# Transposing pairs of bf16 as float32 words in an attention score kernel

## The chip, the cores and the metric

One core of a Trainium2 chip runs the kernel. The metric is the device time of one execution in microseconds (us), as a median over several executions. The profile covers one execution, and its span is somewhat shorter than the time, 201.3 us against about 202.8. A run counts as fast when it is within 1.5% of the fastest of its kernel, and fast runs alone are compared.

The engines: PE does matmuls and transposes, DVE (VectorE) and ACT (ScalarE) copy results out of PSUM, the memory into which PE writes, POOL (GpSimd) casts, and SP issues the transfers that 16 DMA engines carry out. The granted clock is the share of its full clock that the profile shows for PE.

## The reference

```python
batch, heads, seq, dim = 8, 8, 512, 64          # q, k: float32
scale = 1.0 / np.sqrt(q.shape[-1])
return (np.einsum('bhqd,bhkd->bhqk', q, k) * scale).astype(np.float32)
```

Inputs are 2 x 8.39 MB, and the output is 67.11 MB. There is no softmax: everything computed is also written.

## The kernel before

Two batches form a unit, and there are four units. For each, q and k are loaded (4.19 MB), cast to bf16 by POOL, transposed by PE in blocks of 128x128, and copied out of PSUM into `kT` and `qz`. Each unit then has four output buffers. Each takes eight score tiles of 128x1024, filled by two matmuls, and one store of 4.19 MB. The transposes of the next unit are interleaved with the scores of the current one.

```python
big_pool   = ctx.enter_context(tc.tile_pool(name="big", bufs=3))     # loads AND output buffers
tpsum_pool = ctx.enter_context(tc.tile_pool(name="tpsum", bufs=2, space=bass.MemoryType.PSUM))
psum_pool  = ctx.enter_context(tc.tile_pool(name="psum", bufs=3, space=bass.MemoryType.PSUM))
...
# load_and_cast: contiguous bf16
xb = bf_pool.tile([P, J, 2, D], bf16, name="xb")
for s in range(2):
    pinned(nc.gpsimd.tensor_copy(out=xb[:, :, s, :],
                                 in_=xf[:, x, s].rearrange("p (j d) -> p j d", j=J)))
...
# transpose: eight bf16 blocks to a one-bank PSUM tile, then four copies out of it
for j0 in range(0, J, 8):
    tp = tpsum_pool.tile([P, 8, P], bf16, name="tp")
    for j in range(8):
        pinned(nc.tensor.transpose(out=tp[:, j, :], identity=identity, in_=...))
    yield
    yield from rearrange(tp, ...)       # four copies, all on DVE or all on ACT
...
# scores: two matmuls to a tile, one evacuation of 128x1024
ps = psum_pool.tile([P, 2, S], f32, name="ps")
for w in range(2):
    pinned(nc.tensor.matmul(out=ps[:, w, :], lhsT=qz[:, i + w, n, :], rhs=..., ...))
evacuate(o[:, x, i:i + 2, :], ps)       # ACT or DVE, in turn
```

`pinned` keeps each engine's program order. The three `big` buffers serve the four loads first and the sixteen output buffers after that. So an early output buffer waits for a cast to empty it, and a later one for a store to land. Evacuation, the copy of a filled score tile out of PSUM into an output buffer, goes to ACT, DVE, ACT, ACT, DVE, DVE in turn.

## Time and profile before

| | before |
|---|---|
| time, median of 3 | 202.77 us (202.71 to 202.97) |
| moved by DMA | 83.89 MB, 98.1% of the span of 16 engines |
| DVE / ACT / PE busy | 126.4 / 100.7 / 99.2 us |
| store, issue to landing | 21.4 us |
| copies out of the transposes | 128 of 64x512, 687 ns on DVE, 578 ns on ACT |
| casts | 16, 1896 ns each |

### The profile page before, as it was taken

Reading aid. Unit: us, or ns where it says so; the run is one execution under the profiler, and the core shown is the slowest. Engines: PE = TensorE matmul, PEld = TensorE weight load, DVE = VectorE, ACT = ScalarE, POOL = GpSimd, SP = SyncE. Lnnn points to the kernel's source line nnn. Section 1 sums busy time; section 2 is a strip of 40 time slices with the busy share of each in tenths; the row PEclk is TensorE's granted clock in tenths of the full one; section 3 lists DMA queues with packets and bytes.
Section 4 is the critical chain, followed back from the end, with each engine's and each line's share of the span. In section 5 each row is a group of like instructions: output and inputs, shape, how many; then the busy total and the mean of one; then the engine's idle time right before and its main releaser. Section 6 shows DMA issues by size and latency. Waiting matters only on the chain.

```text
span 201.3 us, 1456 instructions
## 1 busy us (share of the span) xinstructions
PE 99.2 (49%) x503; PEld 48.3 (24%) x512; DVE 126.4 (63%) x130; ACT 100.7 (50%) x129; POOL 30.6 (15%) x22
## 2 busy tenths in 40 slices
PE   0033366753976729463729554856535666710000
PEld 0033353321522414231315221432212222200000
DVE  6726659995989929796749796569635264530000
ACT  2016667786674856583837663856515341510000
POOL 1277777556000000000000000000000000000000
PEclk9999999998599996999975998888995857555555
DMA  6999999999999999999999999999999999999993
GB/s 205 430 443 430 420 433 440 420 407 427 433 436 425 422 443 427 430 423 440 430 423 433 433 430 427 440 430 423 433 436 430 410 446 433 420 423 433 433 427 163
DMA packets 5510, 83.97 MB, mean 417 GB/s; under 512 B 384, under 2 KB 384, under 8 KB 384
## 3 DMA queue, kind: packets, MB, share of 16 engines
q1 hardware_dynamic: 5504, 83.89, 98.1%
q8 instruction: 4, 0.07, 0.1%
q14 instruction: 2, 0.02, 0.0%
HBM read 16.78 MB, written 67.11 MB: 417 GB/s over the span
## 4 chain that ended last, share of the span: by engine, by line
DMA 63%; DVE 16%; PE 3%; POOL 3%; ACT 1%; POOLq 1%; issue 1%; SPq 0%; DVEq 0%; ACTq 0%
DMA out_dram<-big 43%; DMA big<-in_q_dram 20%; DVE big L66 12%; PE ps L132 3%; DVE qz L95 3%; POOL xb L82 3%; DVE kT L95 1%; ACT big L64 1%; POOLq L186 1%; SPq L78 0%; DVEq L66 0%; SPq L137 0%; ACTq L64 0%; POOLq L82 0%
## 5 line engine op out<-in xcount | busy, mean ns | idle before, releaser
L132 PE MATMUL ps<-kT,qz 128*128 128x512 bf16 x247 | 81.1, 450 | 55.1 <-ACT big L64 39.2
L66 DVE TENSOR_SCALAR big<-ps 128x1024 f32<-128x1024 f32 x64 | 76.3, 1222 | 39.9 <-DMA out_dram<-big 29.1
L64 ACT ACTIVATE big<-ps 128x1024 f32<-128x1024 f32 x64 | 63.7, 1023 | 57.0 <-DMA out_dram<-big 30.8
L132 PEld LDWEIGHTS <-qz 128*128 128x128 bf16 x256 | 27.5, 111 | 96.0 <-issue 83.2
L82 POOL CAST xb<-big 128x2048 bf16<-128x2048 f32 x16 | 29.9, 1896 | 17.6 <-DMA big<-in_k_dram 11.9
L95 DVE COPY kT<-tp 64x512 bf16<-64x512 bf16 x32 | 22.0, 687 | 6.3 <-PE tp L107 5.7
L95 ACT COPY kT<-tp 64x512 bf16<-64x512 bf16 x32 | 18.5, 578 | 14.7 <-PE tp L107 14.4
L95 DVE COPY qz<-tp 64x512 bf16<-64x512 bf16 x32 | 22.0, 687 | 3.1 <-PE tp L116 2.7
L95 ACT COPY qz<-tp 64x512 bf16<-64x512 bf16 x32 | 18.5, 578 | 3.9 <-PE tp L116 3.6
L107 PE MATMUL tp<-identity,xb 128*128 128x128 bf16 x128 | 12.0, 254 | 16.5 <-POOL xb L82 12.5
L116 PE MATMUL tp<-identity,xb 128*128 128x128 bf16 x128 | 12.8, 265 | 6.0 <-DVE kT L95 3.5
L107 PEld LDWEIGHTS <-xb 128*128 128x128 bf16 x128 | 10.5, 116 | 20.8 <-POOL xb L82 12.8
L116 PEld LDWEIGHTS <-xb 128*128 128x128 bf16 x128 | 11.3, 122 | 10.9 <-issue 8.9
L147 DVE MEMSET qz<- 128x4096 uint32 x2 | 6.9, 3472 | 2.5 <-PEq L175 1.7
L95 ACT ACT_TABLE_LOAD x1 | 1.3, 1283 | 0.7 <-PEq L175 0.7
masks.py:199 POOL TENSOR_SCALAR_AFFINE_SELECT identity<-identity 128x128 bf16<-128x128 bf16 x1 | 0.3, 294 | 0.1
masks.py:197 POOL MEMSET identity<- 128x128 bf16 x1 | 0.2, 205 | 0.3 <-POOLq L175 0.3
L175 POOL MEMSET const-float32-0.0<- 128x1 f32 x1 | 0.1, 99 | 0.2 <-issue 0.2
L175 POOL MEMSET const-bfloat16-1.0<- 128x1 bf16 x1 | 0.1, 102 | 0.0
L175 POOL MEMSET const-uint8-127<- 128x1 uint8 x1 | 0.1, 102 | 0.0
L175 POOL MEMSET const-float32-1.0<- 128x1 f32 x1 | 0.1, 99 | 0.0
## 6 DMA issues: line engine op xcount, KB each, us to landing
out_dram<-big SPq DMA_DIRECT2D x16, 4096.0 KB, 21.4
big<-in_k_dram SPq DMA_DIRECT2D x4, 2048.0 KB, 19.2
big<-in_q_dram SPq DMA_DIRECT2D x4, 2048.0 KB, 24.2
```

The costliest lines, as they stand in the source:

```text
L64: pinned(nc.scalar.mul(out=dst, in_=src, mul=scale))
L66: pinned(nc.vector.tensor_scalar(out=dst, in0=src, scalar1=scale, scalar2=None, op0=mybir.AluOpType.mult))
L82: pinned(nc.gpsimd.tensor_copy(out=xb[:, :, s, :], in_=xf[:, x, s].rearrange("p (j d) -> p j d", j=J)))
L95: pinned(copy(out=dst(s, h), in_=src[:, h]))
L107: pinned(nc.tensor.transpose(out=tp[:, j, :], identity=identity, in_=kb[:, j0 + j].rearrange("p s d -> p (s d)")))
L116: pinned(nc.tensor.transpose(out=tp[:, i, jj, :], identity=identity, in_=qb[:, RO * jj + i0 + i].rearrange("p s d -> p (s d)")))
L132: pinned(nc.tensor.matmul(out=ps[:, w, :], lhsT=qz[:, i + w, n, :], rhs=kT[:, n].rearrange("d m s j -> d (m s j)"), start=True, stop=True))
L147: nc.vector.memset(qz, 0.0)
L175: nc = _bacc.Bacc("TRN2", target_bir_lowering=False, num_devices=1)
L186: with _tile.TileContext(nc) as tc:
```

## The change

The intent is to halve the copies. A float32 word that holds two bf16 values is transposed as a unit, so one copy of 512 words carries what two copies of 512 bf16 carried. For this the cast must place two rows side by side, element by element, which makes it write bf16 at a stride of two. A transposed tile doubles from 2 KB per partition, one PSUM bank, to two. The kernel before uses 2 x 1 + 3 x 2 = 8 banks; to stay at eight, one score tile goes. Evacuation then alternates between ACT and DVE, and the steps of the transposes are placed anew between the scores.

```diff
-    psum_pool = ctx.enter_context(tc.tile_pool(name="psum", bufs=3, space=bass.MemoryType.PSUM))
+    psum_pool = ctx.enter_context(tc.tile_pool(name="psum", bufs=2, space=bass.MemoryType.PSUM))
-        if n_evac % 6 in (0, 2, 3):
+        if n_evac % 2 == 0:
             pinned(nc.scalar.mul(out=dst, in_=src, mul=scale))
...
-            xb = bf_pool.tile([P, J, 2, D], bf16, name="xb")
+            xb = bf_pool.tile([P, JP, 2, D, 2], bf16, name="xb")
+            wide = (1, RO)[x]
             for s in range(2):
-                pinned(nc.gpsimd.tensor_copy(out=xb[:, :, s, :],
-                                             in_=xf[:, x, s].rearrange("p (j d) -> p j d", j=J)))
+                pinned(nc.gpsimd.tensor_copy(
+                    out=xb[:, :, s].rearrange("p (g i) d e -> p g e i d", i=wide),
+                    in_=xf[:, x, s].rearrange("p (g e i d) -> p g e i d", e=2, i=wide, d=D)))
...
-        for j0 in range(0, J, 8):
-            tp = tpsum_pool.tile([P, 8, P], bf16, name="tp")
+        for j0 in range(0, JP, W):                 # JP = J / 2, W = 8
+            tp = tpsum_pool.tile([P, W, P], f32, name="tp")
...                                                # the same for q; identity becomes float32
-                take(ahead, 1 + (t > 0 if v == 0 else n % 4 == 3))
+                take(ahead, 1 if v == 0 else int(n in (0, 2, 3, 5, 6)))
```

## The prediction

> **What bounds the kernel now.** I read the busy table first, then the slices, the DMA queues, the chain that ended last and the waits of the queue's own engine.
>
> ```profile
> PE 99.2 (49%) x503; PEld 48.3 (24%) x512; DVE 126.4 (63%) x130; ACT 100.7 (50%) x129; POOL 30.6 (15%) x22
> ...
> DMA  6999999999999999999999999999999999999993
> GB/s 205 430 443 430 420 433 440 420 407 427 433 436 425 422 443 427 430 423 440 430 423 433 433 430 427 440 430 423 433 436 430 410 446 433 420 423 433 433 427 163
> ...
> q1 hardware_dynamic: 5504, 83.89, 98.1%
> ...
> DMA 63%; DVE 16%; PE 3%; POOL 3%; ACT 1%; POOLq 1%; issue 1%; SPq 0%; DVEq 0%; ACTq 0%
> ```
>
> No compute engine is above 63% of the span, while the 16 DMA engines are at 9 tenths or more in every slice but the first and the last, and their packets fill 98.1% of the span: at most 1.9% of 201.3 us, 3.8 us, is not transfer, and that is the first latency and the tail. The work is 83.89 MB, fixed by the inputs and the float32 output. So the bound is the DMA.
>
> How far is compute ahead of it? The page's issue part and the chain in order of time answer that:
>
> ```profile
> out_dram<-big SPq DMA_DIRECT2D x16, 4096.0 KB, 21.4
> ```
>
> ```profile
> 60.06 3.50 DVE big L66 x3
> 63.56 0.02 SPq L137
> 63.58 0.03 issue
> 63.61 20.21 DMA out_dram<-big
> 83.82 0.03 issue
> 83.85 0.05 DVEq L66
> 83.90 0.05 issue
> 83.95 1.23 DVE big L66
> ```
>
> A store of 4 MB takes 4.19 MB / 0.43 GB per ms, some 9.7 us, yet lands 21.4 us after its issue: when a store is issued, about one more is queued ahead of it, and evacuation then waits for a buffer that a store must free (in the waits, DVE stands 29.1 us and ACT 30.8 us for a store to land). The reserve per store is some 21.4 - 9.7 = 11.7 us. In the timeline the first stores are issued at 38.2, 46.1, 58.3 and 63.6 us. Counting back in steps of 9.7 us from the landing at 83.8 us of the fourth, stores land at 54.6, 64.4 and 74.1 us; so the second store had 54.6 - 46.1 = 8.5 us in hand, the third 64.4 - 58.3 = 6.1 us, the fourth 10.5 us. The first had least: all four loads, without it, end near 43 us, so some 4.8 us. The last store is issued at 178.2 us, when about 12 us of older traffic is left.
>
> **What the Trainium skill says.** "DMA: Bandwidth & Descriptors", section "Where 436 GB/s comes from", gives 435 GB/s as the ceiling of the DMA ports of a core; the slices of this trace show 407 to 446, so the queue runs at it and no rearrangement of engines adds to it. "VectorE: DVE Perf Modes", section "Why PSUM operands drop a tier", says that a float32 operand in PSUM keeps VectorE at one element per cycle. The trace has the bf16 copies at 687 ns for 512 elements, about one per cycle too, so a copy of 512 words should cost the same and carry twice the data. "TensorE: Matmul & The Clock Gate", section "Weight-path perf modes — Fast Weight Load (FWL) and DoubleRow", says that the fast weight load is off for FP32 weights; the kernel before loads only bf16 weights, so its trace can't show the float32 price. "SBUF — State Buffer", section "Door 1: The DMA port swizzle", has a note that lines are 16 bytes and that at least two hits per line keep full rate, so that eight bf16 elements is a free stride. The cast will write bf16 at a stride of two elements. No strided cast is in this trace.
>
> **The change, part by part.**
>
> ```profile
> L66 DVE TENSOR_SCALAR big<-ps 128x1024 f32<-128x1024 f32 x64 | 76.3, 1222 | 39.9 <-DMA out_dram<-big 29.1
> L64 ACT ACTIVATE big<-ps 128x1024 f32<-128x1024 f32 x64 | 63.7, 1023 | 57.0 <-DMA out_dram<-big 30.8
> ...
> L82 POOL CAST xb<-big 128x2048 bf16<-128x2048 f32 x16 | 29.9, 1896 | 17.6 <-DMA big<-in_k_dram 11.9
> L95 DVE COPY kT<-tp 64x512 bf16<-64x512 bf16 x32 | 22.0, 687 | 6.3 <-PE tp L107 5.7
> L95 ACT COPY kT<-tp 64x512 bf16<-64x512 bf16 x32 | 18.5, 578 | 14.7 <-PE tp L107 14.4
> ```
>
> *Copies.* 128 copies of 64x512 bf16 become 64 copies of 64x512 words at the same estimated 687 and 578 ns. DVE loses 32 x 0.687 = 22 us, ACT 32 x 0.578 = 18.5 us. That is all off the path, except in the prologue, where copies lie in series with the transposes (13.6 to 29.4 us): four bursts of copies in place of eight, so scores start some 4 to 6 us earlier. The first output buffer is freed only by the cast of the second load, at 27.1 us, so the first store gains about 2 us at most, into a queue that is full anyway.
>
> *Transposes.* 256 of bf16 become 128 of float32. Eight took 0.61 us in the timeline, 76 ns apart. Without the fast load, and with weights that may not be loaded ahead, I guess 200 to 300 ns each, a burst of eight 1.6 to 2.4 us, in PE's program order ahead of the next scores.
>
> *Score tiles.* With three, the fourth store's tile, which had no copies beside it, was filled in 63.6 - 58.3 = 5.3 us: four DVE evacuations of 1.23 us back to back. With two, and evacuation strictly alternating, each engine owns one tile: evacuation 1.23 us, then two matmuls 0.61 us, then about 0.1 us of signals, 1.95 us a round, so 4 x 1.95 = 7.8 us for an output buffer. The remaining copies (0.69 us) fit into the refill gap of 0.7 us. One burst per output buffer adds 1.6 to 2.4 us less the half microsecond or so that PE has idle in a round: 9 to 10 us while the next unit is prepared, 7.8 us in the last unit (up to 9 at the low clock).
>
> *Against the queue.* A store takes 9.7 us. Filling at 9 to 10 us runs about level with it, and a burst of 10.5 us for eight buffers would eat 8 x 0.8 = 6.4 us of a reserve of 10 to 12. The last unit earns it back. So the sum on the path that sets the end is zero.
>
> *Casts.* Sixteen as before. At 1.9 us each nothing moves. POOL has 4.9 us per load of 2 MB for two casts of 3.75 us, so up to about 2.4 us each would still be hidden.
>
> **The rivals.**
> 1. *The strided casts are slow.* At 3.8 us each POOL would need 16 x 3.8 = 61 us from 8.7 us, so the last ends at 69.5, not 48.8. The first store waits for the eighth cast, at 39.1 us, and is issued near 48; the loads end at 43; the second and third stores also come late, some 5 us each. The end: about 216 us. Against it: [...]the note on 16-byte lines. I give it some 6%.
> 2. *Compute becomes the bound.* A float32 transpose at 500 ns makes a burst of 4 us and a fill of 11.3 us. Twelve such and four of 8.5 from a start near 27 us end at 197 us, plus 9.7 us of the last store and 2 us of latency: 208 us. Against it: it needs both the pessimistic transpose and a low clock all along. 3%.
> 3. *Less engine time makes it faster.* For it: 40 us of copies go. Against it: all of it is in engines that already wait for stores. To gain 2% (4 us), transfers would have to outrun 435 GB/s, as only 3.8 us of the span is free of them. 1%.
> 4. *A small shift in the mix.* Around the first store the rate fell to 408 GB/s between 38.3 and 46.1 us, where loads and stores mix. An earlier first store lengthens the mix by about 2 us at 5% loss: 0.1 us.
>
> **Range and chances.** The center is the time before, 202.77, with 0.1 us either way for the mix: 202.8 us. Nothing pulls below 202.2, as the transfers alone hold the queue. The upper end leaves room for a short dry spell at one early store, about 1 us: 204.0. Faster 0.01, within 2% 0.92, slower 0.07, the sum of rivals 1 and 2 with some taken off for partial cases.
>
> **What would show it.** Right: slices of DMA still at 9 tenths from the second on; store landings still 9.7 us apart; DVE near 104 us and ACT near 82 us busy; 64 copies at 687 and 578 ns; casts at 1.9 us; more waits of evacuation on PE and of PE on evacuation than before, and fewer on stores; a shorter time from issue to landing, below 21.4 us, as the reserve shrinks. Wrong: a slice of DMA below 9 tenths between 38 and 70 us (casts), or a steady gap between stores above 9.7 us with PE or DVE at its end (transposes or the two score tiles), or casts above 2.4 us. A fill that outlasts 10.6 us on average would make my prediction wrong even with the casts unchanged.

## The result, and the profile after

The changed kernel takes **202.56 us** (202.40 to 202.63, 4 runs) against 202.80 for the kernel before on the same chip. The ratio is 0.9986, with a 95% interval of 0.9969 to 1.0003: the same. A ratio here is the mean time of one kernel's fast runs over that of the other's fast runs in the same rounds, so it is not quite the ratio of the medians quoted. The result is correct.

The same parts of the page, now of the changed kernel: the busy row, the DMA in 40 slices, the queue's share, and the issue row of the stores.

```profile
PE 105.3 (52%) x384; PEld 45.8 (23%) x384; DVE 106.8 (53%) x98; ACT 85.0 (42%) x97; POOL 39.5 (20%) x22
...
DMA  6999999999999999999999999999999999999994
GB/s 206 424 444 437 421 421 441 434 395 421 434 424 441 428 431 431 433 426 434 431 428 424 434 441 424 431 431 434 424 431 434 431 424 431 428 437 428 428 428 199
...
q1 hardware_dynamic: 5504, 83.89, 98.3%
...
out_dram<-big SPq DMA_DIRECT2D x16, 4096.0 KB, 20.7
```

DVE lost 19.6 us of work and ACT 15.7 us, POOL gained 8.9, and the DMA row has not changed: full from the second slice to the last but one. A store still lands 20.7 us after its issue, so one more is still queued ahead of it.

The costliest groups of the changed kernel. The columns are the line, engine and operation, what is written from what, then busy us and mean ns, then idle time before and its main cause.

```profile
L68 DVE TENSOR_SCALAR big<-ps 128x1024 f32<-128x1024 f32 x64 | 78.4, 1224 | 59.8 <-PE ps L141 37.2
L66 ACT ACTIVATE big<-ps 128x1024 f32<-128x1024 f32 x64 | 65.5, 1023 | 73.0 <-PE ps L141 37.2
...
L89 POOL CAST xb<-big 128x2048 bf16<-128x2048 f32 x16 | 38.8, 2468 | 7.9 <-DMA big<-in_k_dram 7.3
L117 PE MATMUL tp<-identity,xb 128*128 128x128 f32 x64 | 11.6, 346 | 13.4 <-POOL xb L89 13.4
...
L103 DVE COPY kT<-tp 64x512 f32<-64x512 f32 x16 | 11.0, 686 | 6.3 <-PE tp L117 6.0
```

A copy of 512 words costs what a copy of 512 bf16 did, 686 ns, and there are half as many. The cast takes 2468 ns instead of 1896. The main cause of idle time ahead of evacuation has also changed: before, DVE and ACT stood mostly for a store to land (29.1 and 30.8 us); now they stand 37.2 us each for PE to fill a score tile. Why that is shows in the chain that ended last, here in order of time (start us, us, what), while the fourth output buffer is filled:

```profile
59.13 1.24 DVE big L68
60.37 0.04 issue
60.41 0.61 PE ps L141 x2
61.02 0.02 issue
61.04 1.24 DVE big L68
```

DVE owns one score tile and ACT the other. DVE empties its tile in 1.24 us, only then may PE refill it (0.61 us), and only then can DVE go on: a round of 1.91 us. This buffer took from the third store to the fourth, 56.5 to 64.2 us, 7.7 us; the kernel before filled its own in 5.3 us (58.3 to 63.6), with three of its four DVE evacuations back to back in 3.50 us. The slices above show that the queue did not run dry for it.

The first stores are issued at these times (us from the start of the span). The last column is when the queue would run dry without that store. It is an estimate from the bytes moved. For the first row, the eight windows of 5 us up to 40 us average 402 GB/s before and 403 after, so 16.1 MB are through by 40 us, and the 16.78 MB of loads end near 41.6 us. The other rows are counted in the same way.

| store | before | after | dry at about |
|---|---|---|---|
| first | 38.2 | 36.8 | 41.6 |
| second | 46.1 | 47.5 | 51.6 |
| third | 58.3 | 56.5 | 61.5 |
| last | 178.2 | 178.1 | |

Both kernels hold a reserve of some 3 to 5.5 us at these early stores. So the question for the experiments is whether the parts of the change are really hidden one by one, or merely cancel, and how much of that reserve is left.

### The profile page after: what moved, and what is told of

Same layout as the page of the kernel before. It is cut to its first block, busy times and chain, and to the rows that moved or that the text cites. A ratio compares the mean times of both kernels' runs of the same rounds, so it can differ in the third digit from the quotient of the medians.

```text
span 200.7 us, 1143 instructions
## 1 busy us (share of the span) xinstructions
PE 105.3 (52%) x384; PEld 45.8 (23%) x384; DVE 106.8 (53%) x98; ACT 85.0 (42%) x97; POOL 39.5 (20%) x22
## 3 DMA queue, kind: packets, MB, share of 16 engines
q1 hardware_dynamic: 5504, 83.89, 98.3%
HBM read 16.78 MB, written 67.11 MB: 418 GB/s over the span
## 4 chain that ended last, share of the span: by engine, by line
DMA 40%; DVE 10%; PE 8%; ACT 6%; issue 1%; ACTq 0%; SPq 0%; DVEq 0%
DMA out_dram<-big 40%; DVE big L68 9%; PE ps L141 8%; ACT big L66 5%; ACT qz L103 1%; DVE qz L103 1%; ACTq L66 0%; SPq L146 0%; DVEq L68 0%
## 5 line engine op out<-in xcount | busy, mean ns | idle before, releaser
L141 PE MATMUL ps<-kT,qz 128*128 128x512 bf16 x256 | 87.6, 447 | 55.5 <-ACT big L66 41.6
L68 DVE TENSOR_SCALAR big<-ps 128x1024 f32<-128x1024 f32 x64 | 78.4, 1224 | 59.8 <-PE ps L141 37.2
L66 ACT ACTIVATE big<-ps 128x1024 f32<-128x1024 f32 x64 | 65.5, 1023 | 73.0 <-PE ps L141 37.2
L141 PEld LDWEIGHTS <-qz 128*128 128x128 bf16 x256 | 27.2, 106 | 111.0 <-issue 97.5
L89 POOL CAST xb<-big 128x2048 bf16<-128x2048 f32 x16 | 38.8, 2468 | 7.9 <-DMA big<-in_k_dram 7.3
L117 PE MATMUL tp<-identity,xb 128*128 128x128 f32 x64 | 11.6, 346 | 13.4 <-POOL xb L89 13.4
L103 ACT COPY kT<-tp 64x512 f32<-64x512 f32 x16 | 9.2, 577 | 15.3 <-PE tp L117 15.1
L103 DVE COPY kT<-tp 64x512 f32<-64x512 f32 x16 | 11.0, 686 | 6.3 <-PE tp L117 6.0
L117 PEld LDWEIGHTS tp<-identity,xb 128*128 128x128 f32 x64 | 10.5, 184 | 15.2 <-POOL xb L89 13.4
L103 DVE COPY qz<-tp 64x512 f32<-64x512 f32 x16 | 11.0, 687 | 2.7 <-PE tp L125 2.5
L103 ACT COPY qz<-tp 64x512 f32<-64x512 f32 x16 | 9.6, 602 | 2.9 <-PE tp L125 2.7
L125 PE MATMUL tp<-identity,xb 128*128 128x128 f32 x64 | 9.4, 300 | 2.5 <-ACT kT L103 2.5
L125 PEld LDWEIGHTS tp<-identity,xb 128*128 128x128 f32 x64 | 8.5, 156 | 4.3 <-issue 3.3
## 6 DMA issues: line engine op xcount, KB each, us to landing
out_dram<-big SPq DMA_DIRECT2D x16, 4096.0 KB, 20.7
```

What stands on the lines that cost most here:

```text
L66: pinned(nc.scalar.mul(out=dst, in_=src, mul=scale))
L68: pinned(nc.vector.tensor_scalar(out=dst, in0=src, scalar1=scale, scalar2=None, op0=mybir.AluOpType.mult))
L89: pinned(nc.gpsimd.tensor_copy(out=xb[:, :, s].rearrange("p (g i) d e -> p g e i d", i=wide), in_=xf[:, x, s].rearrange("p (g e i d) -> p ...
L103: pinned(copy(out=dst(s, h), in_=src[:, h]))
L125: pinned(nc.tensor.transpose(out=tp[:, i, jj, :], identity=identity, in_=qb[:, RO * jj + i0 + i]))
```

## The experiments

Twelve kernels ran, each timed over three rounds beside the kernel before. The theory: the DMA queue sets the time, and every part of the change is hidden as long as the stores stay ahead of it. The rival: fewer copies gain, and slower casts and a lost score tile lose, by about as much.

### Each part alone

**a_plain_cast**: the changed kernel with the old contiguous cast. Its numbers are wrong, since the wrong elements are paired.

```diff
-            xb = bf_pool.tile([P, JP, 2, D, 2], bf16, name="xb")
+            xb = bf_pool.tile([P, J, 2, D], bf16, name="xb")
...                                          # contiguous cast as before, viewed as words
```

> The changed kernel with the old contiguous cast (numbers wrong on purpose: pairs are packed in the wrong order). Theory: casts are 1.9 us again in place of 2.47, POOL waits for loads again, and the time stays 202.3 to 202.9. Rival (the slower casts cost some of the gain): below 202.0 us.

Measured: 202.65 us (202.44 to 202.67), ratio to the kernel before 0.9988 (0.9971 to 1.0004). Casts are 1896 ns again and POOL stands idle 15.7 us, nearly all for loads, in place of 7.9, and the time is that of the changed kernel. The slower casts cost nothing here.

```profile
L89 POOL CAST xb<-big 128x2048 bf16<-128x2048 f32 x16 | 29.9, 1896 | 15.7 <-DMA big<-in_k_dram 10.9
```

**b_two_scores**: the kernel before with two score tiles and alternating evacuation, bf16 transposes kept.

```diff
-    psum_pool = ctx.enter_context(tc.tile_pool(name="psum", bufs=3, ...))
+    psum_pool = ctx.enter_context(tc.tile_pool(name="psum", bufs=2, ...))
-        if n_evac % 6 in (0, 2, 3):
+        if n_evac % 2 == 0:
```

> The kernel before with two score tiles and strictly alternating evacuation, bf16 transposes kept. Theory: 202.4 to 203.1 us, no change; the reserve of a store (issue to landing) falls from 21.4 us to some 18 to 20. Rival of cancelling parts: the loss alone shows, 205 us or more.

Measured: 202.96 us (202.94 to 203.17), ratio 1.0005 (0.9990 to 1.0020). Issue to landing fell to 19.7 us, so the loss is real, and it comes out of the reserve and not out of the time.

```profile
out_dram<-big SPq DMA_DIRECT2D x16, 4096.0 KB, 19.7
```

Two parts taken singly, neither moves the time: they do not cancel, they are hidden. The third part, word transposes and fewer copies with their steps placed anew, is what separates a_plain_cast from b_two_scores, which have the same cast times, score tiles and evacuation order: 202.65 against 202.96 us, 0.15%.

**a_three_scores**: the changed kernel with three score tiles, for which one transposed tile has to go.

```diff
-    tpsum_pool = ... name="tpsum", bufs=2 ...      psum_pool = ... name="psum", bufs=2 ...
+    tpsum_pool = ... name="tpsum", bufs=1 ...      psum_pool = ... name="psum", bufs=3 ...
```

> The changed kernel with three score tiles in PSUM again, paid for with one transposed tile in place of two. Theory (the DMA queue sets the time, all of the change is hidden): 202.4 to 202.9 us, the same as the changed kernel; waits of evacuation on the scores fall well below the 37 us each of the changed kernel. Rival (gains of fewer copies and losses of two score tiles cancel on the path): with the loss undone it is faster, below 200 us.

Measured: 207.33 us (206.10 to 208.51), ratio 1.0217 (1.0172 to 1.0263): longer without doubt, though the interval leaves open whether by 2%. Both theories missed it. The DMA in slices of this run:

```profile
DMA  6999999949899999999999999999999999999994
GB/s 214 440 424 440 427 430 427 424 191 414 351 456 411 408 459 408 422 438 411 434 427 414 443 424 414 446 421 424 434 418 424 427 418 440 424 418 440 427 430 191
```

The ninth slice, which starts at 41 us, is down to 191 GB/s: the queue ran dry after the loads. The first store was issued at 43.7 us, past the 41.6 us at which the loads end. The timeline of its prologue says why (start us, us, engine, line, operation, count, then idle before and what ended it):

```profile
13.48 1.97 PE L117 MATMUL tp<-identity,xb 128*128 128x128 f32 x8 [13.48 <-POOL xb L89]
15.48 2.79 DVE L103 COPY kT<-tp 64x512 f32<-64x512 f32 x4 [6.08 <-PE tp L117]
...
18.42 1.94 PE L117 MATMUL tp<-identity,xb 128*128 128x128 f32 x8 [2.98 <-DVE kT L103]
20.40 2.35 ACT L103 COPY kT<-tp 64x512 f32<-64x512 f32 x4 [18.39 <-PE tp L117]
```

With one transposed tile each burst waits for the copies of the burst before, and the first score evacuation moves from 28.1 to 32.2 us. Waits on the scores did fall, to 20.1 us on DVE and 32.3 on ACT. This run changed two pools.

**a_one_tp**: the changed kernel with one transposed tile, its two score tiles kept.

> The changed kernel with one transposed tile and its two score tiles: the other half of the edit that made a_three_scores 4.8 us slower. Theory (the single transposed tile puts bursts and copies of the prologue and of unit 0 in series, so that the first store misses the end of the loads at some 41.6 us): first store issued at 44 to 46 us, 206 to 211 us. Rival (three score tiles slow the kernel by themselves, say by the clock or the order of evacuation): 202.3 to 203 us.

Measured: 208.15 us (207.61 to 208.78), ratio 1.0249 (1.0221 to 1.0276), first store at 43.7 us, just before the 44 to 46 that I expected. So the single transposed tile by itself makes the kernel miss the end of the loads. The third score tile did not cause that loss. The change paid for its two-bank transposed tiles with the right pool.

### How much reserve is left

**a_one_more_cast**: the changed kernel, one of the four casts of each unit issued twice.

```diff
+                for _ in range(2 if x == 0 and s == 0 else 1):
                     pinned(nc.gpsimd.tensor_copy(...))
```

> The changed kernel with one of four casts of each unit issued twice: 4 more of 2.47 us, so POOL ends at about 58 us in place of 48. Theory (a store has a reserve of 5 to 8 us, then the delay goes through in full): the third store, freed by the last cast, is issued near 65.7 us, 1 to 3 us after the second one ends: 203.5 to 206 us. Rival (casts are hidden whatever their length): 202.6 us.

Measured: 208.80 us (208.31 to 209.12), ratio 1.0288 (1.0269 to 1.0308). Casts are not hidden whatever their length: 9.9 us more of them cost about 6 us. My figure was too low. The third store was issued where I expected it (65.2 us). The first, at 41.8, met the end of the loads, and the second, at 55.4, came well after the first store's bytes:

```profile
DMA  6999999989299999999999999999999999999994
GB/s 213 444 419 444 416 447 413 438 346 432 105 457 406 428 435 406 451 409 416 441 406 438 425 425 438 413 432 432 419 438 416 428 428 425 428 419 432 432 425 197
```

The loss sits in the ninth and the eleventh slice. In windows of 5 us from 40 to 60 us the rates are 347, 419, 213 and 338 GB/s. Against 427 that is (80 + 8 + 214 + 89) / 427 x 5 = 4.6 us of the 5.8 us by which the span grew.

**a_casts_twice**: every cast issued twice.

> The changed kernel with every cast issued twice: 32 of 2.47 us from 8.6 us, POOL ends at 87.6 us. Theory: the queue runs dry before each of the first three stores (evacuation of the first starts at 48, of the second at 67.8, of the third at 87.6 us): some 33 us lost, 230 to 239 us. Rival (casts are hidden): 202.6 us.

Measured: 238.98 us (238.71 to 239.06), ratio 1.1766 (1.1747 to 1.1786). The first two stores were issued at 57.3 and 78.6 us. Once the reserve is spent, POOL's time goes through to the end, as expected.

### What the change does to the compute path

Hidden work cannot be read from the time. So the bound was lifted: these four kernels store one row in eight and leave most of the output unwritten (wrong).

```diff
-        nc.sync.dma_start(out=out_r[v, t], in_=o.rearrange("p x i k -> p x (i k)"))
+        nc.sync.dma_start(out=out_r[v, t][:, :, 0:S], in_=o[:, :, 0, :])
```

**b_small_store**, the kernel before:

> The kernel before storing one row in eight (most of the output is left unwritten on purpose), so that stores no longer bound it and the compute path shows. Loads and casts last until 48.8 us as before, then units 1 and 2 at some 33 us each (16 evacuations of 1.22 and 16 copies of 0.69 us are 30.6 us of DVE), unit 3 at 21 us, after some 58 us for unit 0. Expected: 145 to 158 us.

**a_small_store**, the changed kernel:

> The changed kernel storing one row in eight. My theory: though it has 22 us less DVE and 18 us less ACT work, its path is not shorter, as each score tile is now evacuated in a round of 1.95 us: 8.6 to 9.5 us per output buffer in units 1 and 2, 7.8 in unit 3, after some 64 us: 160 to 174 us, slower than the kernel before with small stores. Rival (less engine work is a shorter path that the DMA hides): faster than the kernel before with small stores, 130 to 145 us.

**b_small_two**, the kernel before with two score tiles:

> The kernel before storing one row in eight, with two score tiles. Theory: the score tiles alone lengthen the path; DVE rounds of 1.95 us plus those of 16 copies that do not fit in the gap: 35 to 40 us for units 1 and 2, 31 for unit 3: 165 to 178 us, slower than the kernel before with small stores by over 10 us. Rival: within 3 us of it.

**a_small_three**, the changed kernel with three score tiles and one transposed tile:

> The changed kernel storing one row in eight, with three score tiles and one transposed tile. Theory: the rounds of 1.95 us go, evacuation runs back to back, DVE needs 16 x 1.22 + 8 x 0.69 = 25 us in a unit, so units of 26 to 29 us and 20 to 22 for the last: 132 to 148 us, faster than the kernel before with small stores. Rival (the float32 transposes or casts are what lengthens the path): no faster than the changed kernel with small stores.

The spacing of stores is taken from the issue times: units 1 and 2 from the fourth to the twelfth store divided by 8, unit 3 from the twelfth to the last divided by 4.

| kernel, small stores | time, us | per buffer, units 1, 2 | per buffer, unit 3 |
|---|---|---|---|
| b_small_store | 148.90 (148.30 to 149.26) | 7.2 | 6.4 |
| a_small_store | 165.35 (165.29 to 165.47) | 8.3 | 7.7 |
| b_small_two | 167.64 (167.57 to 167.74) | 8.3 | 8.1 |
| a_small_three | 154.05 (153.63 to 155.01, three fast runs) | 7.8 | 5.1 |

The granted clocks of the four profiles are close (1.00, 0.95, 0.98 and 0.98).

The changed kernel does some 34 us less DVE and ACT work, and its compute path is **16.5 us longer**. The busy rows of b_small_store and then a_small_store show the exchange:

```profile
PE 88.4 (60%) x503; PEld 43.4 (30%) x512; DVE 125.1 (85%) x130; ACT 100.8 (69%) x129; POOL 30.5 (21%) x22
```

```profile
PE 92.6 (57%) x377; PEld 46.9 (29%) x384; DVE 106.8 (65%) x98; ACT 85.0 (52%) x97; POOL 39.5 (24%) x22
```

DVE at 85% was near to being the limit of the compute path; at 65% it stands idle in the rounds. The waits of the two kernels (us in total, times, longest), b_small_store first:

```profile
ACT big L64 <- PE ps L132: 20.1, 27, 1.8
DVE big L66 <- PE ps L132: 3.0, 4, 0.9
```

```profile
ACT big L66 <- PE ps L141: 50.3, 47, 3.5
DVE big L68 <- PE ps L141: 32.0, 42, 3.3
```

DVE waits 32.0 us for scores in place of 3.0, which is more than the 18.3 us of its work that went. Taking one score tile from the kernel before, with evacuation alternating, is enough to produce this: b_small_two is 18.7 us slower than b_small_store, and at 8.3 us per buffer it equals the changed kernel. With two score tiles, saved copies only lengthen the idle time. With three (a_small_three) unit 3 runs at 5.1 us a buffer, near the 4 x 1.23 = 4.9 us of DVE alone. It alternates too, so the alternation is not what costs. It even fills faster than the order of the kernel before: the last three buffers, with three score tiles and no copies in both, are 4.9 us apart here and 5.8 in b_small_store, where DVE does three evacuations back to back and then stands 0.7 to 0.9 us. Its total, still above b_small_store and above what I expected, includes the slow prologue of one transposed tile: its second store leaves at 50.7 us against 42.4.

**b_two_big** and **a_two_big**: the kernel before and the changed one with two large buffers, so that no second store can be queued while a buffer is being filled.

```diff
-    big_pool = ctx.enter_context(tc.tile_pool(name="big", bufs=3))
+    big_pool = ctx.enter_context(tc.tile_pool(name="big", bufs=2))
```

> The kernel before with two of the large buffers in place of three, so that the reserve of a queued store is gone: a period for two stores is the larger of 19.5 us and one filling plus some 12.7 us. With a filling of about 8.3 us in units 1 and 2 and 5.3 to 6 in unit 3, and about 4.5 us of a dry queue early on: 209 to 217 us.

> The changed kernel with two of the large buffers. Theory (its filling of an output buffer is longer, 8.5 to 9.5 us in units 1 and 2, 7.8 in unit 3): 3 to 7 us slower than the kernel before with two buffers, 213 to 222 us. Rival (less engine work fills faster): faster than the kernel before with two buffers by 2 us or more.

Measured: b_two_big 213.12 us (212.67 to 213.86), ratio 1.0501 (1.0476 to 1.0525), and a_two_big 216.61 us (216.11 to 218.21), ratio 1.0682 (1.0640 to 1.0725). Issue to landing is 12.5 and 12.1 us, so little is queued. Now, with the full output written, the changed kernel is 3.5 us (1.6%) the slower of the two. The third large buffer hides this, but it is not the score tiles alone. Between 40 and 60 us the rates are 323 and 257 GB/s, which at 427 is some 3.1 us (an estimate): the first store leaves at 46.9 us in place of 44.3. Its buffer is freed by a cast 1.4 us later (at 38.01 against 36.66 us), and takes 8.9 us to fill in place of 7.7. No run separates the two.

## Why the prediction was right

**The bound.** It held: DMA is full in every slice but the first and last, 98.3% of the span. The landings stay 9.7 us apart where evacuation waits for them. Most slices lie near the 435 GB/s of the prediction, but the page that it cites has a lower limit beside it (see the last section).

**Copies.** Right: 64 copies at 686 ns on DVE and 577 to 602 on ACT; DVE ended at 106.8 us where I said near 104, ACT at 85.0 where I said near 82. The remainder of the busy time is mainly evacuation rows that the page of before counts at slightly less than 64 times their mean. The scores started 3.6 us earlier (23.6 in place of 27.2 us), a little less than the 4 to 6 that I gave, and the first store left 1.4 us earlier.

**Transposes.** Mis-sized on the safe side: nine of the sixteen bursts of eight took 1.04 us, below my 1.6 to 2.4. Three took 1.68 to 1.92 us at a granted clock of 0.50 to 0.61. The first two took 3.68 us together; the page shows a clock of 1.00 for them, but the trace has no clock record before 17.4 us. The 76 ns in the prediction are a burst of eight divided by eight; from start to start, as one takes 0.22 us in bf16 and 0.27 us in words, it is (0.61 - 0.22) / 7 = 56 ns and (1.04 - 0.27) / 7 = 110 ns. So half as many transposes cost PE about the same.

**Score tiles.** Right in the mechanism: rounds of 1.91 us where I had 1.95, and, with small stores, 7.7 us per buffer in unit 3 where I had 7.8. In units 1 and 2 it was 8.3 and not 9 to 10, most likely as the bursts were shorter, and filling stayed ahead of the 9.7 us of a store. The waits moved in part as I said: on scores from 6.4 to 37.2 us on DVE and from 20.8 to 37.2 on ACT; on stores from 29.1 to 15.5 on DVE, but on ACT they stayed (30.8 and 31.3). PE did not wait more for evacuation (54.0 us before, 53.1 after). None of this reached the queue.

**Casts.** This term was wrong. I took 1.9 us and gave slow casts some 6%; it was 2.47, just past the 2.4 us that I had given as the limit of what is hidden. POOL ran fourteen casts without a pause, and even so the last ended at 48.0 us, 0.8 us earlier than before: the last load landed earlier, and POOL could start on it at 43.2 us in place of 45.1. Why it landed earlier is not shown, and I had not foreseen it. a_plain_cast shows no cost, a_one_more_cast shows that 9.9 us more is not free; nothing in between was run.

**The reserve.** Too large at the early stores, by reading landings as the end of a store's bytes. I gave the second 8.5 us and the third 6.1; counted by bytes it was 5.5 and 3.2, since the next store has already begun when one lands. The first had 3.4, not 4.8. The same slip made my expectation for a_one_more_cast too low.

**Rivals.** Slow casts came true in part, at 2.47 and not 3.8 us. Compute as the bound did not come true, though the path did grow by 16.5 us under the stores. Less engine time making it faster stayed at nothing measurable.

What stays open is whether the 0.24 us between the medians is real. The interval includes 1. The kernels with word transposes and two transposed tiles (the changed one and a_plain_cast) lie 0.2 to 0.3 us below the kernel before, and b_two_scores does not; no run was made to settle a tenth of a per cent.

## What to carry to other kernels

When the queue of transfers is full in every slice, judge a change by how early stores are issued against the moment the queue would run dry, counted in bytes, and not by busy time saved. A buffer pool that is one tile short turns saved engine work into idle rounds. To see what a hidden change did to the compute path, shrink the transfers and time both kernels again; here that showed a longer path that the full kernel did not reveal.

## What the Trainium skill lacked or had wrong

- "DMA: Bandwidth & Descriptors", section "Where 436 GB/s comes from", which the prediction cites for the 435 GB/s, also says that transfers between HBM and SBUF are held to about 358. Here, with one core running, they moved 418 GB/s over the whole span.
- "SBUF — State Buffer", section "Door 1: The DMA port swizzle", has the note that bf16 may be stepped by up to eight elements at full rate. The cast on POOL that writes bf16 at a stride of two took 2468 ns against 1896 contiguous, with 2048 elements in both: 30% more. The order in which the cast walks the tile changed too, and no run separates that from the stride.
- "TensorE: Matmul & The Clock Gate", section "Weight-path perf modes — Fast Weight Load (FWL) and DoubleRow", excludes FP32 from the fast load without a duration for a float32 transpose. Here eight of 128x128 took 1.04 us (110 ns from start to start) at a granted clock of 1.00 and 1.68 to 1.92 us at 0.50 to 0.61; eight of bf16 took 0.61 us (56 ns) at 1.00. Whether the weight load makes the difference is not shown.
- I found no page with the cost of a score tile too few when evacuation alternates between two engines: 7.7 us for an output buffer in place of 5.3, and 18.7 us of compute path in b_small_two.
